# Three PSUM banks for the scores and two for the row maxima, in place of two and three

## The chip, the core and the metric

The kernel runs on one NeuronCore of a Trainium2 chip. The metric is the device time of one execution in microseconds (us). TensorE multiplies matrices and writes its results into PSUM, which has eight banks of 128 partitions by 512 fp32 values. VectorE (DVE in the profile) and ScalarE (ACT) read the results from there; GpSimd (POOL) works on SBUF alone, and SyncE (SP) issues nearly all DMAs. Each engine takes its instructions in one fixed order, and waits on semaphores for the others.

## What is computed

One step of a small hybrid decoder: one recurrent layer, then one attention layer ("FoX", attention with a forget term) on 2048 new prompt tokens, and the same for 8 sequences of 8 sampled tokens with 4096 cached positions each. The attention has 16 heads of 64 dimensions. All values are fp32. Cut to the attention:

```python
def fox_block(q, k, v, cq, ck, q_pos, k_pos):
    s = jnp.einsum('bqhd,bkhd->bhqk', q, k).astype(jnp.float32) * (HEAD_DIM ** -0.5)
    s = s + jnp.swapaxes(cq, 1, 2)[:, :, :, None] - jnp.swapaxes(ck, 1, 2)[:, :, None, :]
    mask = k_pos[None, :] <= q_pos[:, None]
    s = jnp.where(mask[None, None], s, -jnp.inf)
    p = jax.nn.softmax(s, axis=-1)
    return jnp.einsum('bhqk,bkhd->bqhd', p.astype(v.dtype), v)
```

`c` is the running sum of the log-forget values. The result is gated with `silu(g)`, multiplied with the output weights, normalized and added to the residual.

## The kernel before

**Stages.** Up to about 1240 us of the span the recurrent layer and the first half of the projections to queries, keys, values and gates run; up to about 1705 us come the other projections, beside the decode attention over the cached pages. From about 1705 us to 2842 us the prompt's attention runs (`attention`), and until about 2725 us the rest of the decode attention runs beside it, its pages streaming in from the cache. Then the last rows of the output projection end the program.

**The prompt's attention.** The work is cut into 64 units: one head `h` and one block `qc` of 512 queries, with qc running 0, 1, 2, 3 in even heads and 3, 2, 1, 0 in odd ones. A unit has 4(qc+1) tiles of 128 keys by 512 queries. For each unit:

- Row maxima first (`top`, L1405 to L1422). For each 128 queries and each block of 512 keys TensorE writes approximate scores, queries on the partitions, into a PSUM tile `sx` (L1415, one fp32r matmul of up to 512 columns). DVE reduces it to one maximum for each query: L1417 for whole blocks, L1419 with a mask on the diagonal. When a unit's last `sx` is reduced, DVE takes the maximum over the blocks (L1428), TensorE transposes the four columns into a PSUM tile `mps` (L1432), and ACT writes them, negated, in four steps as rows 96 to 99 of the query operand `qbt` (L1434).
- Scores (L1552 to L1555). For each tile of 128 keys TensorE adds up in a PSUM tile `st`: L1552 with `qa`, `ka`, which needs no maxima; L1553 with `qbt`, `kbt`, which brings in the forget term and subtracts the row maxima, so that it needs the unit's L1434; and L1555, the causal mask, on the diagonal. ACT takes the exponential (L1561) into `p`, or into `acc` for the first tile.
- Products with the values (L1572, `ops`), for four tiles together; POOL adds the `p` tiles into `acc` (L106) for the sums of the softmax.
- `total` (L1465, PSUM tile `tot`) sums `acc` over the partitions, and `norm` and `gate` (L1489, PSUM tile `rp`) scale and gate the result and send it to DRAM (`ogd`).

**The decode beside it.** For a page of keys, SP's queue brings `raw` (L1083), DVE transposes it (L1168, `ktr`), TensorE forms scores (L1136, `dS`) and DVE subtracts and reduces; for a page of values TensorE multiplies (L1246, `dO`). It has two PSUM banks of its own, tags `d` and `o`.

**PSUM.** The attention's pool has six banks: one for `ops`, two under the tag `st`, three under the tag `sx`. The tag `sx` serves `sx`, `mps`, `tot` and `rp` in turn. A tile that takes a bank waits until its last owner has been read. Once the decode is done (`dec_done`), `scores_bank` (L1536) takes every other score tile from the decode's two banks, so that there are four in turn.

**The order.** The program is written as generators that call each other. `advance` (L1507) writes the maxima tiles some 18 ticks, of one score tile each, ahead of the scores that need them, and `Side` deals out the decode's steps along the attention's. That is not the order of the engines, though: the framework's scheduler plays the program through on a clock of its own, and puts an instruction into its engine's order when its inputs and its buffer are free there. The number of banks thus sets the order. `behind` (L110) keeps the transposes of L1168 behind the last row maximum on DVE, and the products `dS` and `dO` behind the last score matmul on TensorE.

**The last rows.** `project` (L1617) multiplies 17 blocks of rows with the output weights. Even blocks take their two PSUM tiles `y` from the decode's banks, odd ones from the tag `st` (L1661).

Of the kernel before, what the change touches and what calls it, by code (L numbers as in the profile page):

```python
# [11 lines left out]
F32 = mybir.dt.float32  # L12
# [73 lines left out]
def tile_hawk_fox(  # L86
# [1231 lines left out]
    def attention(es):  # L1318
# [1 line left out]
        ps3 = psum["att"]  # L1320

        ops2 = ps3.tile([P, 512], F32, name="ops", tag="ops", bufs=1)
        ps3.tile([P, 512], F32, name="st", tag="st", bufs=2)
        pool.tile([P, 512], F32, name="acc", tag="acc", bufs=NACC)
        pool.tile([P, 512], F32, name="p", tag="p", bufs=NP)
        pool.tile([P, 512], F32, name="oT", tag="oT", bufs=5)
# [78 lines left out]
        def top(u, j, ck):  # L1405

            h, qc = units[u]
            assert h in loaded and u < done[1]
            kb, qb = kbs[h % 2], qbs[u % NQ]
            if (j, ck) == (0, 0):  # L1410
                mxs[u] = small.tile([P, 4, 4], F32, name="mxs", tag="mxs")
            mx = mxs[u]
            w = 512 if ck < qc else (j + 1) * P
            ps = ps3.tile([P, 512], F32, name="sx", tag="sx", bufs=3)
            T.matmul(ps[:, :w], qb[0:96, j * P:(j + 1) * P], kb[0:96, ck * 512:ck * 512 + w], start=True, stop=True)  # L1415
            if ck < qc:
                place["V"] = V.reduce_max(mx[:, j, ck:ck + 1], ps[:, :w], axis=AX.X).ins  # L1417
            else:
                V.tensor_tensor_reduce(ps[:, :w], ps[:, :w], maskb[:, 512 - w:], scale=1.0, scalar=NEG,  # L1419
                                       op0=ALU.add, op1=ALU.max, accum_out=mx[:, j, ck:ck + 1])  # L1420
            if j == 3 and ck == qc:
                later.after(1, lambda: tops(u))  # L1422

        def tops(u):

            h, qc = units[u]
            m = mrows[u % 2]
            V.tensor_reduce(m[:, :4], mxs.pop(u)[:, :, :qc + 1], axis=AX.X, op=ALU.max)  # L1428

            def row():  # L1430
                ps = ps3.tile([P, 512], F32, name="mps", tag="sx", bufs=3)
                T.transpose(ps[:, :P], m[:, :], ident[:, :])  # L1432
                for j in range(4):
                    A.mul(qbs[u % NQ][96:100, j * P:(j + 1) * P], ps[:4, :P], less[:, j:j + 1])  # L1434

            later.after(1, row)
# [23 lines left out]
        def total(h2, sums, todo, single):  # L1460


            ps = ps3.tile([P, 512], F32, name="tot", tag="sx", bufs=3)
            for qc, acc in todo:
                T.matmul(ps[qc * 32:(qc + 1) * 32, :], ones[:, :32], acc[:, :], start=True, stop=True)  # L1465
            cs = pool.tile([P, 512], F32, name="cs", tag="cs")
            rows = slice(0, P) if len(todo) == 4 else slice(qc * 32, (qc + 1) * 32)
            A.copy(cs[rows, :], ps[rows, :])
            if single:
                for qc, acc in todo:  # L1470
                    j = qc * 2 + h2
                    S.dma_start(sums[j * 16:(j + 1) * 16, :], cs[qc * 32:qc * 32 + 1, :].rearrange("o (r c) -> o r c", r=16))
            else:
                S.dma_start(sums[h2 * HD:(h2 + 1) * HD, :], cs[:, :].rearrange("(q z) (r c) -> z q r c", z=32, r=16)[0])

        def norm(pr, sums, q0, n, oT):

            ps_ = slice(q0 * 32, (q0 + n) * 32)
            V.reciprocal(sums[ps_, :], sums[ps_, :])
            rs = [pool.tile([P, 32], F32R, name=f"rs{x}", tag=f"rs{x}") for x in range(2)]  # L1480
            V.tensor_copy(rs[0][ps_, :], sums[ps_, :])
            tt(V, rs[1][ps_, :], sums[ps_, :], f(rs[0][ps_, :]), ALU.subtract)
            for x in range(2):
                to = rr[x * 8:(x + 1) * 8, :] if n == 4 else rr[x * 8 + q0:x * 8 + q0 + 5:4, :]
                S.dma_start(f(to).rearrange("j (r c) -> j r c", r=16), f(rs[x][ps_, :]))

            def gate(qc, sg):
                ps = ps3.tile([P, 512], F32, name="rp", tag="sx", bufs=3)
                T.matmul(ps[:, :], sel[:, qc, :], rr[:, :], start=True, stop=True)  # L1489
                tt(G, sg[:, :], sg[:, :], oT[qc - q0][:, :], ALU.mult)  # L1490
                tt(V, sg[:, :], sg[:, :], ps[:, :], ALU.mult)
                S.dma_start(og_d[qc][pr * P:(pr + 1) * P, :], sg[:, :])

            def fetch(qc):
                sg = pool.tile([P, 512], F32, name="sgt", tag="sgt", bufs=2)
                S.dma_start(sg[:, :], sg_d[pr * P:(pr + 1) * P, qc * 512:(qc + 1) * 512])
                later.after(3, lambda: gate(qc, sg))

            for qc in range(q0, q0 + n):
                later.after((3 if n == 4 else 0) + 2 * (qc - q0), lambda qc=qc: fetch(qc))  # L1500
# [35 lines left out]
        def scores_bank():  # L1536

            if dec_done:
                wide[0] += 1
                if wide[0] % 2:  # L1540
                    return psum["dec"].tile([P, 512], F32, name="st", tag="do"[wide[0] // 2 % 2], bufs=1)
            return ps3.tile([P, 512], F32, name="st", tag="st", bufs=2)

        for u, (h, qc) in enumerate(units):
            load_low(u + 2)
# [71 lines left out]
    def project(es):  # L1617

        bpostB, out = proj["g"], proj["out"]

        def tiled(t):
            return t.rearrange("p (k t) -> p k t", k=KB)

        def gated_rows(i, og):
            m, t, res, _ = rows[i]
            if t is None:
                tt(V, og[:, :, :m], oTs[:, :, :], sgs[:, :, :], ALU.mult)
            else:
                S.dma_start(og[:, :, :], og_d[t // 512][:, t % 512:t % 512 + P].rearrange("(k p) t -> p k t", p=P))

        def residual(i, x1):
            m, t, res, _ = rows[i]
            S.dma_start(x1[:m, :], res)

        def split(i, og, oh, ol):
            m = rows[i][0]
            cp(A, oh[:, :, :m], og[:, :, :m])
            tt(V, ol[:, :, :m], og[:, :, :m], f(oh[:, :, :m]), ALU.subtract)

        def post(i, pool, yps, x1, y):  # L1640
            m, t, res, dst = rows[i]
            ss = sumsq(pool, yps, m)
            r = rsqrt(ss[:m], m, 0.25 / D, post=0.5)
            for j in range(2):
                sl = slice(j * 512, (j + 1) * 512)
                V.scalar_tensor_tensor(y[:m, sl], yps[j][:m, :], r[:m, 0:1], bpostB[:m, sl], op0=ALU.mult, op1=ALU.mult)
                tt(V if i == len(rows) - 1 and j == 1 else G, y[:m, sl], y[:m, sl], x1[:m, sl], ALU.add)
                if i == len(rows) - 1:
                    S.dma_start(dst[:, sl], y[:m, sl])
            if i < len(rows) - 1:  # L1650
                S.dma_start(dst, y[:m, :])

        pool = sbuf(es, "proje", "right")
        hs = lent["halves"]()
        sets = [dict(og=pool.tile([P, KB, P], F32, name="ogT"), x1=pool.tile([P, D], F32, name="x1"),
                     oh=pool.tile([P, KB, P], F32R, name="ohT"), ol=pool.tile([P, KB, P], F32R, name="olT"),
                     y=pool.tile([P, D], F32, name="yo"),
                     ps=lambda j: psum["dec"].tile([P, 512], F32, name="y", tag="do"[j], bufs=1)),
                dict(og=tiled(lent["res"][:, :D]), x1=lent["res"][:, D:], oh=tiled(hs[:, :D]), ol=tiled(hs[:, D:]),
                     y=lent["out"][:, :, :].rearrange("p k d -> p (k d)"),  # L1660
                     ps=lambda j: lent["psum"].tile([P, 512], F32, name="y", tag="st", bufs=2))]  # L1661

        def part(i, fn, *names):
            if i < len(rows):
                fn(i, *(sets[i % 2][n] for n in names))

        for i in range(2):
            part(i, gated_rows, "og")
            part(i, residual, "x1")
        part(0, split, "og", "oh", "ol")  # L1670
        for i in range(len(rows)):
            b = sets[i % 2]
            yps = []
            for j in range(2):
                ps = b["ps"](j)
                out.product(ps, rows[i][0], j, b["oh"], b["ol"])
                yps.append(ps)
                if j == 0:
                    part(i + 2, gated_rows, "og")
                    part(i + 1, split, "og", "oh", "ol")  # L1680
            post(i, pool, yps, b["x1"], b["y"])
            part(i + 2, residual, "x1")
            if i == 3:
                later.flush()
# [175 lines left out]
```

## Time and profile before

| | us |
|---|---|
| median of 3 runs (3048.39 to 3065.48) | 3050.73 |
| the profiled execution | 3044.43 |
| its span, first to last instruction | 3042.6 |
| TensorE busy in the span | 2818.0 (93%) |
| DVE busy | 1801.1 (59%) |
| ACT busy | 1271.1 (42%) |
| POOL busy | 1080.0 (35%) |
| attention beside the decode, 1705 to 2725 us: span / TensorE busy | 1020.0 / 939.6 |
| attention alone, 2725 to 2842 us | 117.0 / 110.4 |
| last rows, from 2842 us | 200.6 / 190.9 |

The profile is one execution. A matmul's time in a row is its way through the array, and matmuls follow each other faster than that; the distance of two starts says how long one holds TensorE. "PEld" is the load of a matmul's stationary operand, which overlaps the matmuls before it. "PEclk" is the TensorE clock that was granted, as a share of full speed. "idle before <- X" is the time that an engine stood idle before a group, and what ended it. Some fp32 matmuls are shown as two.

### The profile page before, as it was taken

To read this page: it belongs to the slowest core of one execution; us is meant where nothing else is said; L and a number is where in the kernel's file an instruction comes from. 1 tells how busy PE (TensorE), PEld (TensorE's weight loads), DVE (VectorE), ACT (ScalarE), POOL (GpSimd) and SP (SyncE) were. 2 spreads that over 40 slices of the span, in tenths; PEclk is the share of its full clock that TensorE was granted. 3 is DMA by queue.
4 is the path that set the end of the run, shared out by engine and by line. 5 is a ranking of instruction groups with operands and counts; after the bars stand their busy time and mean duration, and the time that the engine had idled before them with its cause. 6 is when DMAs were issued, how large, how long until landed. Compare 5 with 4: busy or idle time off the path is not lost.

```text
span 3042.6 us, 60436 instructions
## 1 busy us (share of the span) xinstructions
PE 2818.0 (93%) x21614; PEld 2260.3 (74%) x21614; DVE 1801.1 (59%) x4012; ACT 1271.1 (42%) x2874; POOL 1080.0 (35%) x1199
## 2 busy tenths in 40 slices
PE   5998999999999989998999799899999999999998
PEld 5997789989899978896788455556655656556687
DVE  7876455425357765766555566666666766555344
ACT  4665442222236654433244144344434444355321
POOL 1653201000015532000000265556665666558422
PEclk9999999999999999999999799999999999999999
DMA  4224546788622265999999978898889898974343
GB/s 122 84 83 133 176 123 197 241 263 265 223 91 79 84 195 176 302 327 323 327 311 325 276 229 258 259 273 260 267 270 282 253 278 258 276 232 117 96 146 109
DMA packets 492862, 653.39 MB, mean 215 GB/s; under 512 B 91099, under 2 KB 292828, under 8 KB 485285
## 3 DMA queue, kind: packets, MB, share of 16 engines
q1 hardware_dynamic: 488934, 643.87, 67.8%
q10 hardware_dynamic: 3340, 3.56, 0.5%
q8 instruction: 171, 2.80, 0.4%
q0 software_dynamic: 288, 2.10, 0.2%
q14 instruction: 129, 1.06, 0.1%
HBM read 513.82 MB, written 135.16 MB: 213 GB/s over the span
## 4 chain that ended last, share of the span: by engine, by line
PE 51%; DMA 15%; DVE 6%; ACT 4%; SPq 4%; issue 3%; POOL 1%; ACTq 0%; DVEq 0%; POOLq 0%
PE ops L1572 7%; PE st L1552 4%; PE sx L1415 4%; DMA raw<-in_cache_k_dram 3%; PE dO L1246 3%; PE y L379 3%; PE y L378 3%; PE y L377 3%; PE kv L378 3%; PE kv L377 3%; PE st L1553 3%; PE kv L379 3%; PE dS L1136 3%; DMA raw<-in_cache_v_dram 3%; SPq L1083 2%
## 5 line engine op out<-in xcount | busy, mean ns | idle before, releaser
L106 POOL TENSOR_TENSOR acc<-acc,p 128x512 f32<-128x512 f32 (+3 forms) x576 | 639.7, 1112 | 408.2 <-PE ops L1572 220.6
L1561 ACT ACTIVATE p<-st 128x512 f32<-128x512 f32 (+3 forms) x576 | 291.5, 525 | 398.0 <-PE st L1553 183.9
L1168 DVE STREAM_TRANSPOSE ktr<-raw 128x1024 f32<-128x1024 f32 x256 | 308.0, 1226 | 107.2 <-DMA raw<-in_cache_k_dram 94.4
L1417 DVE TENSOR_REDUCE mxs<-sx 128x1 f32<-128x512 f32 x384 | 254.1, 681 | 183.2 <-PE sx L1415 182.0
L378 PE MATMUL kv<-wl,xh 128*128 128x256 f32 (+3 forms) x1088 | 310.0, 288 | 9.4 <-DVE wl L422 9.3
L377 PE MATMUL kv<-wh,xh 128*128 128x256 f32 (+3 forms) x1088 | 310.5, 290 | 6.9 <-ACT wh L421 6.6
L379 PE MATMUL kv<-wh,xl 128*128 128x256 f32 (+3 forms) x1088 | 309.8, 287 | 0.0
L1552 PE MATMUL st<-qa,ka 128*128 128x512 f32 (+3 forms) x640 | 273.1, 427 | 12.6 <-ACT p L1561 10.9
L1572 PE MATMUL ops<-p,vvt 128*64 128x256 f32 (+1 forms) x2176 | 269.1, 374 | 3.8 <-ACT p L1561 3.6
L1415 PE MATMUL sx<-kbt,qbt 96*128 96x512 f32 (+3 forms) x640 | 233.9, 421 | 34.8 <-DVE mxs L1419 12.7
L421 ACT ACTIVATE wh<-wst,gv 128x256 fp32r<-128x256 f32 (+1 forms) x384 | 164.3, 499 | 184.4 <-DMA wst<-in_b_w_in_dram 69.9
L1553 PE MATMUL st<-qbt,kbt 128*128 128x512 f32 (+3 forms) x640 | 238.1, 373 | 0.0
L422 DVE SCALAR_TENSOR_TENSOR wl<-wst,gv,wh 128x256 fp32r<-128x256 f32 (+1 forms) x384 | 170.2, 493 | 113.5 <-ACT wh L421 110.3
L1572 PEld LDWEIGHTS ops<-p,vvt 128*64 128x64 f32 x2176 | 165.0, 143 | 91.7 <-issue 22.2
L377 PE MATMUL qg<-xh,wh 128*128 128x384 f32 (+2 forms) x640 | 228.3, 358 | 0.0
L379 PE MATMUL qg<-xh,wl 128*128 128x384 f32 (+2 forms) x640 | 226.7, 355 | 1.1 <-DVE wl L422 1.1
L378 PE MATMUL qg<-xl,wh 128*128 128x512 f32 (+2 forms) x640 | 226.6, 356 | 0.0
L378 PEld LDWEIGHTS kv<-wl,xh 128*128 128x128 f32 (+1 forms) x1088 | 204.0, 189 | 13.9 <-DVE wl L422 10.9
L1101 POOL TENSOR_TENSOR qw<-qb,amask 128x128 f32<-128x128 f32 x64 | 29.4, 463 | 518.1 <-PE dS L1136 276.6
L377 PEld LDWEIGHTS kv<-wh,xh 128*128 128x128 f32 (+1 forms) x1088 | 203.8, 189 | 11.9 <-ACT wh L421 7.5
L379 PEld LDWEIGHTS kv<-wh,xl 128*128 128x128 f32 (+1 forms) x1088 | 205.7, 190 | 4.1 <-issue 3.9
L1552 PEld LDWEIGHTS st<-qa,ka 128*128 128x128 f32 x640 | 125.1, 196 | 107.4 <-issue 54.6
(297 smaller groups left out, 6346.4 us busy)
## 6 DMA issues: line engine op xcount, KB each, us to landing
raw<-in_cache_k_dram SPq DMA_DIRECT2D x512, 256.0 KB
raw<-in_cache_v_dram SPq DMA_DIRECT2D x512, 256.0 KB
wst<-in_w_kv_dram SPq DMA_DIRECT2D x48, 512.0 KB
wst<-in_b_w_in_dram SPq DMA_DIRECT2D x48, 512.0 KB
xt<-in_x_prompt_dram SPq DMA_DIRECT2D x32, 512.0 KB
wst<-in_a_w_in_dram SPq DMA_DIRECT2D x64, 256.0 KB
out_dram<-kf SPq DMA_DIRECT2D x128, 128.0 KB
sc<-cd SPq DMA_DIRECT2D x16, 1024.0 KB
```

What stands on the lines that cost most here:

```text
L106: eng.tensor_tensor(out, a, b, op=op)
L377: T.matmul(ps, lh(k), rh(k), start=(k == 0), stop=False)
L378: T.matmul(ps, lh(k), rl(k), start=False, stop=False)
L379: T.matmul(ps, ll(k), rh(k), start=False, stop=(k == nk - 1))
L422: V.scalar_tensor_tensor(wl[:, k, :], st[:, k, :], gk, f(wh[:, k, :]), op0=ALU.mult, op1=ALU.subtract)
L1168: behind("V", V.transpose(t.kts[pp][:, n], raw[:, :, pp * 256:(pp + 1) * 256]).ins)
L1415: T.matmul(ps[:, :w], qb[0:96, j * P:(j + 1) * P], kb[0:96, ck * 512:ck * 512 + w], start=True, stop=True)
L1417: place["V"] = V.reduce_max(mx[:, j, ck:ck + 1], ps[:, :w], axis=AX.X).ins
L1552: place["T"] = T.matmul(ps[:, lo:], ka[:, ks], qa[:, lo:], start=True, stop=False).ins
L1553: T.matmul(ps[:, lo:], kb[:, ks], qb[:, lo:], start=False, stop=(k < qc * 4))
L1561: pair.append((k, lo, p, A.activation(p[:, lo:], ps[:, lo:], AF.Exp)))
L1572: return T.matmul(ops[r * HD:(r + 1) * HD, a0 * P:], vvs[h % 2][:, k, :], p[:, :].rearrange("p (a r c) -> p a r c", a=2, r=2)[:, a0:, r, : ...
```

## The change

The attention's six banks are dealt out anew: three under the tag `st`, two under the tag `sx`. So that the number of score banks after the decode stays four, `scores_bank` then takes every fourth tile from the decode's bank `d`, and no more from `o`. The odd blocks of the last rows turn through three banks and no longer two.

```diff
@@ attention
-        ps3.tile([P, 512], F32, name="st", tag="st", bufs=2)
+        ps3.tile([P, 512], F32, name="st", tag="st", bufs=3)
@@ top
-            ps = ps3.tile([P, 512], F32, name="sx", tag="sx", bufs=3)
+            ps = ps3.tile([P, 512], F32, name="sx", tag="sx", bufs=2)
@@ tops, row; total and gate have the same for "tot" and "rp"
-                ps = ps3.tile([P, 512], F32, name="mps", tag="sx", bufs=3)
+                ps = ps3.tile([P, 512], F32, name="mps", tag="sx", bufs=2)
@@ scores_bank
                 wide[0] += 1
-                if wide[0] % 2:
-                    return psum["dec"].tile([P, 512], F32, name="st", tag="do"[wide[0] // 2 % 2], bufs=1)
-            return ps3.tile([P, 512], F32, name="st", tag="st", bufs=2)
+                if wide[0] % 4 == 0:
+                    return psum["dec"].tile([P, 512], F32, name="st", tag="d", bufs=1)
+            return ps3.tile([P, 512], F32, name="st", tag="st", bufs=3)
@@ project
-                     ps=lambda j: lent["psum"].tile([P, 512], F32, name="y", tag="st", bufs=2))]
+                     ps=lambda j: lent["psum"].tile([P, 512], F32, name="y", tag="st", bufs=3))]
```

No instruction is added or removed. The orders of the engines in the attention are others, since the scheduler made them anew with the new banks. The rows below are TensorE's order. `qbt_19530` to `qbt_19535` are the six query operands that the units take in turn, so that a name's number tells the unit; two score rows (L1552, L1553) with one `qbt` are one tile of that unit's scores.

The first place is the beginning of the unit of head 12 with qc = 2, whose operand is `qbt_19532`. Before:

```order
L1415 MATMUL sx<-kbt_19529,qbt_19533 128x512 x2
L1415 MATMUL sx<-kbt_19529,qbt_19533 128x384
L1552 MATMUL st<-qa,ka 128x128
L1553 MATMUL st<-qbt_19531,kbt_19529 128x128
L1555 LDWEIGHTS identB
L1555 MATMUL st<-causal,identB 128x128
L1552 MATMUL st<-qa,ka 128x512
L1553 MATMUL st<-qbt_19532,kbt_19529 128x512
L1415 MATMUL sx<-kbt_19529,qbt_19533 128x512
```

After:

```order
L1553 MATMUL st<-qbt_19531,kbt_19529 128x128
L1555 LDWEIGHTS identB
L1555 MATMUL st<-causal,identB 128x128
L1552 MATMUL st<-qa,ka 128x512
L1415 MATMUL sx<-kbt_19529,qbt_19532 128x512 x3
L1432 MATMUL mps<-ident,mrow_19567 128x128
L1415 MATMUL sx<-kbt_19529,qbt_19533 128x512 x2
L1553 MATMUL st<-qbt_19532,kbt_19529 128x512
L1415 MATMUL sx<-kbt_19529,qbt_19533 128x512
```

Before, the unit's first L1553 follows its L1552 at once, and the maxima tiles around it belong to the next unit, 19533. Now the unit's own last three maxima tiles and the transpose of its maxima stand between its L1552 and its L1553.

The second place is the beginning of the unit of head 11 with qc = 3, operand `qbt_19532` with the keys `kbt_19537`, beside which the decode's `dS` and `dO` run. Before:

```order
L1552 MATMUL st<-qa,ka 128x128
L1553 MATMUL st<-qbt_19531,kbt_19529 128x128
L1555 LDWEIGHTS identB
L1555 MATMUL st<-causal,identB 128x128
L1246 MATMUL dO<-raw,sx 32x256 x8
L1415 MATMUL sx<-kbt_19537,qbt_19533 128x512
L1552 MATMUL st<-qa,ka 128x512
L1553 MATMUL st<-qbt_19532,kbt_19537 128x512
L1136 MATMUL dS<-ktr,qw 32x128 x32
```

After:

```order
L1552 MATMUL st<-qa,ka 128x512
L1415 MATMUL sx<-kbt_19537,qbt_19532 128x512 x2
L1415 MATMUL sx<-kbt_19537,qbt_19532 128x384
L1415 MATMUL sx<-kbt_19537,qbt_19532 128x512 x4
L1136 MATMUL dS<-ktr,qw 32x128 x32
L1432 MATMUL mps<-ident,mrow_19567 128x128
L1415 MATMUL sx<-kbt_19537,qbt_19533 128x512
L1246 MATMUL dO<-raw,sx 32x256 x8
L1151 MATMUL dS<-sy,qw 32x8 x16
L1415 MATMUL sx<-kbt_19537,qbt_19533 128x512
L1415 MATMUL sx<-kbt_19537,qbt_19533 128x128
L1553 MATMUL st<-qbt_19532,kbt_19537 128x512 x3
```

The seven last maxima tiles of the unit, which stood more than thirty rows ahead of its scores, have moved down to just before them, seven in a row on two banks. The first halves of three score tiles stand above them (the third is the first row shown), and their three second halves together below.

More of the change, by code (lines that the diff above doesn't have):

```diff
@@ L1460, in total @@
         def total(h2, sums, todo, single):
-            ps = ps3.tile([P, 512], F32, name="tot", tag="sx", bufs=3)
+            ps = ps3.tile([P, 512], F32, name="tot", tag="sx", bufs=2)
             for qc, acc in todo:
@@ L1487, in gate @@
             def gate(qc, sg):
-                ps = ps3.tile([P, 512], F32, name="rp", tag="sx", bufs=3)
+                ps = ps3.tile([P, 512], F32, name="rp", tag="sx", bufs=2)
                 T.matmul(ps[:, :], sel[:, qc, :], rr[:, :], start=True, stop=True)
```

## The prediction

> **What bounds the kernel now.** I read the head of the page first, then the busy time by stage, and then, in the stage of the change, the waits of TensorE, because an engine that is busy for 93% of the span can only be slowed or sped by what it waits for.
>
> ```profile
> span 3042.6 us, 60436 instructions
> PE 2818.0 (93%) x21614; PEld 2260.3 (74%) x21614; DVE 1801.1 (59%) x4012; ACT 1271.1 (42%) x2874; POOL 1080.0 (35%) x1199
> ```
>
> The execution took 3044.43 us around this span. The median of the three runs is 6.3 us more.
>
> ```profile
> core 0: us, PE busy (x) PEld busy (x) DVE busy (x) ACT busy (x) POOL busy (x), PEclk, DMA share, GB/s
> 1705.00:1724.00 19.00, 11.05 (x23) 6.01 (x24) 11.40 (x32) 2.11 (x8) 2.23 (x5) 0.50 1.08 293
> 1724.00:2725.00 1001.00, 928.54 (x8457) 593.08 (x8457) 636.41 (x1341) 437.33 (x1086) 585.50 (x563) 0.95 0.86 263
> 2725.00:2842.00 117.00, 110.38 (x653) 69.02 (x652) 58.34 (x117) 68.99 (x146) 101.79 (x85) 0.97 0.39 107
> 2842.00:3042.60 200.60, 190.87 (x829) 151.14 (x827) 83.00 (x266) 39.47 (x87) 47.07 (x39) 0.99 0.38 122
> ```
>
> The attention beside the decode (1724 to 2725 us) is the stage that counts. TensorE stands idle there for 1001 - 928.5 = 72.5 us. The granted clock is 0.95 on average; as it reads 0.50 in the first row and near 1 in the last, I take it that half speed held for about a tenth of the stage, some 100 us, which cost 50 us of work. DVE is at 64%, ACT at 44%, the DMA at 0.86. What TensorE waited for in this stage:
>
> ```profile
> PE dO L1246 <- DMA raw<-in_cache_v_dram: 19.9, 10, 5.2
> PE sx L1415 <- DVE mxs L1419: 12.4, 11, 5.1
> PE st L1552 <- ACT p L1561: 10.9, 24, 2.3
> PE rp L1489 <- DMA r<-rs: 4.7, 3, 2.7
> PE mps L1432 <- DVE mrow L1428: 4.3, 4, 2.7
> PE sx L1415 <- DVE mxs L1417: 4.2, 8, 1.0
> ```
>
> The banks of the scores cost 10.9 us (L1552 waits until an exponential has freed one), and the banks of the maxima 12.4 + 4.2 = 16.6 us. A wait on a `qbt` before L1553, the point at which the maxima reach the scores, is not among the rows: with three banks the maxima are ready in time. So the first prize is small, and the question is what the third bank of the maxima was worth.
>
> **The price of a maxima tile.** This is one round trip, from the order of time:
>
> ```profile
> 2029.78 0.50 PE L1415 MATMUL sx<-kbt,qbt 96*128 96x512 f32 x1
> 2030.12 0.40 PE L1552 MATMUL st<-qa,ka 128*128 128x512 f32 x1
> 2030.35 1.95 DVE L1417 TENSOR_REDUCE mxs<-sx 128x1 f32<-128x512 f32 x3
> 2030.36 0.39 PE L1553 MATMUL st<-qbt,kbt 128*128 128x512 f32 x1
> 2030.59 0.63 PE L1415 MATMUL sx<-kbt,qbt 96*128 96x512 f32 x2
> 2030.85 0.60 ACT L1561 ACTIVATE p<-st 128x512 f32<-128x512 f32 x1 [0.21 <-PE st L1553]
> ```
>
> ```profile
> L1417 DVE TENSOR_REDUCE mxs<-sx 128x1 f32<-128x512 f32 x384 | 254.1, 681 | 183.2 <-PE sx L1415 182.0
> L1168 DVE STREAM_TRANSPOSE ktr<-raw 128x1024 f32<-128x1024 f32 x256 | 308.0, 1226 | 107.2 <-DMA raw<-in_cache_k_dram 94.4 <-DMA qa<-qd 4.4 <-issue 3.8
> ```
>
> A 512-wide matmul holds TensorE for 0.23 us (from 2030.36 to 2030.59). The reduction starts 0.57 us after its matmul and takes 0.68, so a bank comes back 1.25 us after the matmul's start at the earliest, and later by 1.23 us for every transpose of L1168 that stands ahead on DVE. Of three maxima tiles in a row on two banks the third is due at 0.46 us and waits 0.79; each further one waits for DVE's pace, 0.68 - 0.23 = 0.45.
>
> **Part 1: maxima tiles close behind the last owner of their bank.** I went through TensorE's order before and after, bank by bank, and summed the work between the last write of a bank's owner and the first of the next (0.23 us for 512 columns, 0.24 for a product's pair of rows). Before, 20 maxima tiles have less than 0.3 us between, and 50 have 0.3 to 0.9; after, 101 and 80, and ten more `tot` and `rp` tiles stand right behind maxima. So 81 + 10 new waits of between 0.45 and 0.79 us: 41 to 72 us. I take 0.6, since most are in runs of three or four: 55 us. For the 30 of the middle class the same arithmetic gives 0 to 0.7 us each, 0 to 20; I take 0.27, as much of this distance was already covered before (the 16.6 us were all that 70 close tiles cost): 8 us. Queued behind such a tile is all of TensorE: the scores for which ACT waits, and `dS` and `dO`, which free the page buffers that SP's loads wait for.
>
> **Part 2: the maxima come just in time.** This is what the third score bank does to the order. A score tile's first half (L1552) needs no maxima, so with a free bank it goes ahead, and the maxima tiles, short of banks, fall back. Between a unit's last `sx` and its first L1553 stood a median of 16.7 us of TensorE work, 3.3 at the least. Now it is 5.3, and under 2.9 in 16 of 64 units; in 29 units (3 before) less than 1.4 us stand between `mps` and L1553, and in 10 (4 before) less than 1.4 between the last `sx` and `mps`. What this distance must hold:
>
> ```profile
> 2018.35 0.68 DVE L1419 CUSTOM_DVE_ANT_0 sx<-sx,maskb 128x512 f32<-128x512 f32 x1
> 2018.95 0.13 DVE L1419 DVE_READ_ACCUMULATOR2_ANT mxs<- 128x1 f32 x1
> 2019.12 0.17 DVE L1428 TENSOR_REDUCE mrow<-mxs 128x4 f32<-128x12 f32 x1
> ```
>
> ```profile
> 2024.54 0.33 PE L1432 MATMUL mps<-ident,mrow 128*128 128x128 f32 x1
> 2024.90 1.11 ACT L1434 ACTIVATE qbt<-mps,less 4x128 fp32r<-4x128 f32 x4 [1.80 <-PE mps L1432]
> ```
>
> From a tile's start to its maximum in `mrow` it is 0.57 + 0.94 = 1.5 us (1.3 after TensorE is done with it), and from `mps` to the last write of `qbt` 2026.01 - 2024.54 = 1.47. What is missing to 1.4 us, summed over the units, is 1.2 us before and 21.2 after at `mps` to L1553, and 2.9 and 12.9 at `sx` to `mps`: 30 us more. The bounds are 0, if TensorE is late there anyway, and about 50, if the four writes of L1434 stand behind an exponential of 0.60 us each time (29 x 0.6 = 17). I take 30.
>
> **Part 3: the scores' banks.** Score tiles with less than 0.5 us of work since their bank's last owner fall from 34 to 15. All that can be gained is the 10.9 us; I take 7.
>
> **Part 4: what the DMA waits give back.** A later TensorE finds its pages there: of the 19.9 + 4.7 us of DMA waits I take half, 12; bounds 0 and 24.6.
>
> **Part 5: the clock.** A wait costs more than its length here:
>
> ```profile
> 2012.08 1.94 PE L1415 MATMUL sx<-kbt,qbt 96*128 96x384 f32 x3 [1.87 <-DVE mxs L1419]
> ```
>
> ```profile
> 2012.60:2022.80 10.20, 10.17 (x69) 7.23 (x73) 6.87 (x15) 2.18 (x6) 2.79 (x3) 0.50 0.91 258
> ```
>
> After this wait of 1.87 us for a maxima bank the clock stood at 0.50 for 10.2 us, with TensorE busy all along: 5 us more. Over the stage it is 50 us lost for 72.5 us idle, 0.7 for each; the new waits are shorter than that one, so I take 0.3 of the 55 + 8 + 30 - 7 - 12 = 74 us: 22. The bounds are 0 and 0.7 x 74 = 52.
>
> The Trainium skill, page "TensorE: Matmul & The Clock Gate", section "Loop structure matters more than you think", has reading a result out of PSUM as something that doesn't make TensorE go cold; by that the term would be 0 and the sum 22 us smaller. The row at 2012.08 disagrees, as the wait was for just such a read.
>
> **Edits at nothing.** After the decode, four score banks turn before and after; TensorE is busy for 110.4 of 117 us there, and this rotation hides the exponential equally. The unused bank `o` is missed by nobody until `project` takes it. In the last rows the third bank could only touch the idle 200.6 - 190.9 = 9.7 us, and the next tile's 24 matmuls (5.5 us) cover the reads.
>
> **Sum.** 55 + 8 + 30 - 7 - 12 + 22 = 96 us. Against the profiled execution that is 3044 + 96 = 3140 us, against the median 3147; I name 3140.
>
> **Rivals.**
>
> *The scores' bank decides.* Faster: ACT's waits on scores are the longest of its own, so a third bank might let TensorE run ahead. For it speaks that ACT and DVE both idle longest for TensorE:
>
> ```profile
> ACT p L1561 <- PE st L1553: 179.9, 130, 7.0
> DVE mxs L1417 <- PE sx L1415: 158.2, 95, 7.2
> ```
>
> Against it: both rows say that they wait for TensorE, not it for them. Its price is the 10.9 us at L1552 and, at 0.7, 8 of clock: 3044 - 19 = 3025 us. It decides if the maxima tiles' banks come back in time all the same, that is if parts 1 and 2 realise less than 19 us.
>
> *Hidden behind the page stream.* If the pages at a DMA share of 0.86 set the pace, TensorE's new waits fall into those for pages. Parts 1 and 2 then shrink by the whole 24.6 us, and cost their lower ends, 41 + 0 + 0, with no clock term: 3044 + 41 - 7 - 25 = 3053 us, up to 3065. Against it: pages account for only about 20 of the 72.5 us idle.
>
> *The clock falls.* If every wait counts as the one at 2012.08, with lost work 2.7 times the wait (5 / 1.87), on half of the 93 us of parts 1 and 2: 0.5 x 93 x 2.7 = 126 us in place of 22, and 3244 us. For it speaks that row; against it that the stage's mean is 0.7.
>
> The Trainium skill's same page describes this in the section "A second HAM failure mode: psum-queue depth-cycling": turning through PSUM banks leaves small idle gaps, and the clock swings between half and full. The 3244 us is this rule at work.
>
> **Chances.** The forecast 0.62; hidden 0.17; the clock falls 0.13; the scores' bank decides 0.08. My forecast's own terms reach from 3044 + 41 - 11 - 25 = 3049 to 3044 + 72 + 20 + 50 + 52 = 3238. The range leaves out the faster rival, the lower half of the hidden one and the clock's far end: 3060 to 3215. A measurement of this kernel can tell about 0.5% (15 us) from no change. Faster than 3035 is the first rival alone, 0.08; within 3035 to 3066 lies a little over half of the hidden one, 0.09; the rest, 0.83, is slower.
>
> **What the profile of the changed kernel would show.** Part 1: `sx` waiting on `mxs` goes from 16.6 us to over 50. Part 2: a row of L1553 waiting on `qbt` of L1434 appears, with 15 us or more, and `mps` waiting on `mrow` grows past 10. Part 3: L1552 waiting on `p` falls below 8 us. Part 4: `dO` waiting on `raw` falls. Part 5: PEclk in the stage falls below 0.94. The last rows keep their 200 us. I would be wrong if the waits at L1415 stayed near 17 us, or if they came and the page waits went by the same amount.

## The result, and the profile after

The changed kernel takes 3186.68 us (median of 4 runs, 3171.68 to 3191.84) against 3049.56 us of the kernel before on the same chip. The ratio is 1.0441, with a 95% interval of 1.0412 to 1.0469: it is 137 us slower. The profiled executions differ by 3169.8 - 3042.6 = 127 us of span, and the readings below account for those.

The head of the page after, and the busy time by stage. The decode now ends at about 2837 us and the attention at about 2970 us; these stages answer to 1724 to 2725, 2725 to 2842 and 2842 to 3042.6 us before.

```profile
span 3169.8 us, 60453 instructions
PE 2857.9 (90%) x21614; PEld 2269.9 (72%) x21614; DVE 1810.9 (57%) x4012; ACT 1260.2 (40%) x2874; POOL 1076.6 (34%) x1199
```

```profile
core 0: us, PE busy (x) PEld busy (x) DVE busy (x) ACT busy (x) POOL busy (x), PEclk, DMA share, GB/s
1724.00:2837.00 1113.00, 966.10 (x8444) 605.57 (x8437) 637.58 (x1324) 424.69 (x1080) 586.91 (x564) 0.91 0.78 236
2837.00:2970.00 133.00, 118.13 (x656) 72.76 (x657) 68.97 (x137) 66.75 (x145) 91.29 (x81) 0.92 0.28 78
2970.00:3169.80 199.80, 189.86 (x829) 150.25 (x829) 85.32 (x268) 42.17 (x93) 50.78 (x42) 0.99 0.41 133
```

The attention beside the decode is 112 us longer, the attention alone 16 us, the last rows are as before. In the first of these stages TensorE's idle time went from 72.5 to 1113 - 966.1 = 146.9 us. The granted clock fell from 0.95 to 0.91; read as a share of time at half speed, this is 1001 x 0.05 = 50 us of work lost before and 1113 x 0.09 = 100 us after. With the 74 us of new idle time this adds up to 124 us, for 112, so the clock's part is too large as read: half-speed time in which TensorE was idle anyway counts in it. The busy time measures it better: with the same matmuls it grew by 966.1 - 928.5 = 37.6 us, and 74.4 + 37.6 is 112.

TensorE's waits after the change, from 1724 to 2837 us (total us, times, longest):

```profile
PE dO L1246 <- DMA raw<-in_cache_v_dram: 51.1, 26, 7.7
PE sx L1415 <- DVE mxs L1417: 23.8, 44, 1.2
PE dS L1136 <- DVE ktr L1168: 13.5, 7, 3.6
PE mps L1432 <- DVE mrow L1428: 11.6, 11, 2.2
PE sx L1415 <- DVE mxs L1419: 8.8, 15, 1.2
PE sx L1415 <- DVE sgt L106: 6.6, 3, 3.0
PE dO L1246 <- DMA sx<-pd: 4.9, 2, 4.3
PE sx L1415 <- ACT qbt L1434: 4.7, 7, 1.0
PE tot L1465 <- DVE mxs L1417: 3.4, 5, 1.2
...
PE st L1552 <- ACT p L1561: 2.2, 4, 1.3
```

Of the same list before, three rows that the prediction did not show:

```profile
PE dS L1136 <- DVE ktr L1168: 2.6, 4, 1.2
...
PE sx L1415 <- DVE sgt L106: 1.4, 2, 0.9
...
PE sx L1415 <- ACT qbt L1434: 0.8, 2, 0.6
```

The waits for a maxima bank (the `sx` and `tot` rows shown here and in the prediction) went from 4.2 + 12.4 + 1.4 + 0.8 = 18.8 us to 23.8 + 8.8 + 6.6 + 4.7 + 3.4 = 47.3. No single wait of `sx` or `tot` on `mxs` is longer than 1.2 us; there are many, 74 in the five rows where 23 were. `mps` rose by 7.3, value pages by 31.2, transposed keys by 10.9; L1552 gained 8.7. So less than half of the new idle time stands at the maxima's banks, and more at the page stream, though the DMA share fell from 0.86 to 0.78: the pages are late without the transfers being busier. What SP's queue waited for before it could issue page loads (L1083) shows where they start late; before and then after, in the same stage:

```profile
SPq L1083 <- PE dO L1246: 27.9, 11, 4.7
```

```profile
SPq L1083 <- PE dO L1246: 46.3, 24, 4.0
```

A load waits until a product has freed its page buffer, and TensorE's product is late. On ACT, L1434 waits longer for `mps`, and the exponentials wait less for their scores; in the same stage before:

```profile
ACT p L1561 <- PE st L1555: 160.9, 101, 6.6
...
ACT qbt L1434 <- PE mps L1432: 44.0, 23, 7.2
```

and after:

```profile
ACT qbt L1434 <- PE mps L1432: 146.8, 31, 18.2
ACT p L1561 <- PE st L1553: 138.0, 88, 4.5
...
ACT p L1561 <- PE st L1555: 96.7, 63, 6.8
```

L1434 waits 103 us more, and the two rows of the exponentials (L1553 was 179.9 us before) 106 us less. ACT's idle time has changed its place; that the late maxima hold up exponentials which are ready is not shown by it.

### The profile page after: what moved, and what is told of

Its sections match the earlier page's. It is cut to its first block, busy times and chain, and to the rows that moved or that the text cites. A ratio compares the mean times of both kernels' runs of the same rounds, so it can differ in the third digit from the quotient of the medians.

```text
span 3169.8 us, 60453 instructions
## 1 busy us (share of the span) xinstructions
PE 2857.9 (90%) x21614; PEld 2269.9 (72%) x21614; DVE 1810.9 (57%) x4012; ACT 1260.2 (40%) x2874; POOL 1076.6 (34%) x1199
## 4 chain that ended last, share of the span: by engine, by line
PE 49%; DMA 18%; DVE 8%; SPq 3%; ACT 3%; issue 3%; POOL 1%; ACTq 0%; DVEq 0%; POOLq 0%
PE ops L1572 6%; DMA raw<-in_cache_v_dram 5%; PE st L1552 4%; PE sx L1415 3%; PE dO L1246 3%; PE st L1553 3%; PE y L377 3%; PE dS L1136 3%; PE y L379 3%; PE y L378 3%; DMA raw<-in_cache_k_dram 3%; PE kv L377 3%; PE kv L378 3%; PE kv L379 3%; SPq L1083 2%
## 5 line engine op out<-in xcount | busy, mean ns | idle before, releaser
L1561 ACT ACTIVATE p<-st 128x512 f32<-128x512 f32 (+3 forms) x576 | 283.2, 526 | 344.1 <-PE st L1553 146.7
L1417 DVE TENSOR_REDUCE mxs<-sx 128x1 f32<-128x512 f32 x384 | 258.9, 684 | 222.5 <-PE sx L1415 220.3
L1415 PE MATMUL sx<-kbt,qbt 96*128 96x512 f32 (+3 forms) x640 | 268.8, 452 | 68.5 <-DVE mxs L1417 30.8
L1572 PE MATMUL ops<-p,vvt 128*64 128x256 f32 (+1 forms) x2176 | 264.2, 370 | 2.5 <-ACT p L1561 2.4
L1552 PE MATMUL st<-qa,ka 128*128 128x512 f32 (+3 forms) x640 | 260.9, 416 | 5.0 <-ACT p L1561 2.7
L1415 PEld LDWEIGHTS sx<-kbt,qbt 96*128 96x128 f32 x640 | 128.5, 209 | 164.4 <-DVE mxs L1417 66.6
L1553 PE MATMUL st<-qbt,kbt 128*128 128x512 f32 (+3 forms) x640 | 228.1, 379 | 0.0
L1572 PEld LDWEIGHTS ops<-p,vvt 128*64 128x64 f32 x2176 | 162.4, 141 | 90.2 <-issue 20.6
L1246 PE MATMUL dO<-raw,sx 128*32 128x256 f32 x2048 | 151.6, 420 | 74.3 <-DMA raw<-in_cache_v_dram 53.6
```

Of the source, the lines that this page charges most:

```text
L1246: return T.matmul(op[c:c + 32, :256], sx[:, d, i // 4, a * 4:(a + 1) * 4, :].rearrange("p h q -> p (h q)"), raw[:, d, a * 256:(a + 1) * 25 ...
L1552: place["T"] = T.matmul(ps[:, lo:], ka[:, ks], qa[:, lo:], start=True, stop=False).ins
L1553: T.matmul(ps[:, lo:], kb[:, ks], qb[:, lo:], start=False, stop=(k < qc * 4))
L1561: pair.append((k, lo, p, A.activation(p[:, lo:], ps[:, lo:], AF.Exp)))
L1572: return T.matmul(ops[r * HD:(r + 1) * HD, a0 * P:], vvs[h % 2][:, k, :], p[:, :].rearrange("p (a r c) -> p a r c", a=2, r=2)[:, a0:, r, : ...
```

## The experiments

Theory A says that the order does it: the third score bank lets the scores' first halves go ahead, and the maxima fall behind. Theory B says that the round trip of a maxima bank does it: two banks are too few whatever the order. The medians of the timed runs, and the loss of each changed kernel against its own base, are:

| kernel | us | ratio to the kernel before (95%) | loss against its base |
|---|---|---|---|
| changed | 3186.7 | 1.0441 (1.0412 to 1.0469) | 137 |
| two score banks, two maxima banks | 3197.0 | 1.0484 (1.0441 to 1.0527) | 144 |
| before, order held | 3097.4 | 1.0157 (1.0109 to 1.0206) | |
| changed, order held | 3183.2 | 1.0424 (1.0377 to 1.0471) | 86 |
| before, half reduction | 3028.3 | 0.9927 (0.9898 to 0.9956) | |
| changed, half reduction | 3142.8 | 1.0305 (1.0263 to 1.0348) | 115 |
| before, no decode beside | 2750.7 | 0.9016 (0.8981 to 0.9052) | |
| changed, no decode beside | 2805.7 | 0.9200 (0.9171 to 0.9229) | 55 |
| changed, bank `o` to the maxima after the decode | 3186.8 | 1.0438 (1.0405 to 1.0472) | 135 |
| before, transposes cut | 3064.4 | 1.0053 (1.0028 to 1.0079) | |
| changed, transposes cut | 3172.3 | 1.0421 (1.0378 to 1.0465) | 108 |
| before, half of the value pages | 3033.0 | 0.9949 (0.9930 to 0.9969) | |
| changed, half of the value pages | 3176.0 | 1.0421 (1.0372 to 1.0470) | 143 |

**The maxima bank taken away, nothing given.** On the kernel before:

```diff
-tag="sx", bufs=3
+tag="sx", bufs=2        (sx, mps, tot and rp)
```

> The kernel before with the third maxima bank taken away and nothing given to the scores (two and two, the sixth bank of the pool idle). Theory A, the order: the loss comes from maxima that fall behind because the scores' first halves go ahead into a third bank. Without that bank the first halves stand apart from their second halves in 26 of 64 units (6 before the change, 53 after it), so the loss should be about half: 3100 to 3140 us. Theory B, the round trip: two maxima banks are too few in any order, and the third score bank gained 8 us; the time should be that of the changed kernel and those 8 us: 3185 to 3205 us.

It took 3197.0 us. The whole loss comes from the maxima's bank, as B said, and the third score bank is worth about 10 us, which is within the intervals; the expected 8 us fit. A's figure of 3100 to 3140 us falls, and with it A's mechanism as the main one: first halves stand ahead far less often here (in 26 of 64 units against 53, as the expectation counts them), and the loss was no smaller.

**The order held.** On the changed kernel, and as a control on the kernel before:

```diff
-T.matmul(ps[:, :w], qb[0:96, j * P:(j + 1) * P], ...)
+place["X"] = T.matmul(ps[:, :w], qb[0:96, j * P:(j + 1) * P], ...).ins
...
 place["T"] = T.matmul(ps[:, lo:], ka[:, ks], qa[:, lo:], start=True, stop=False).ins
+behind("X", place["T"])
```

> The changed kernel (three score banks, two maxima banks) with TensorE's order held: a score tile's first half may not stand ahead of the maxima tiles that the program wrote before it. The median distance from a unit's last maxima tile to its first second half is then 25 us of TensorE's work (16 before the change, 5 after it); maxima tiles within 0.3 us of their bank's last owner are 64 (21 before, 103 after), within 0.3 to 0.9 us 250 (57 and 88). Theory A, the order: most of the loss is back, 3050 to 3090 us, and the waits for pages are near those of before (20 us). Theory B, the round trip: the close tiles still wait, and 250 middling ones with them: 3150 us or more.

> The kernel before (two score banks, three maxima banks) with the same hold on TensorE's order; the median distance is 27 us in place of 16. The control for the held order alone. Theory A: the distance was enough already, so no change or a little less: 3030 to 3060 us. Theory B: the maxima tiles' own waits do not change (13 close tiles in place of 21): 3040 to 3060 us. Over 3070 us would say that the hold costs something by itself, and the other held run is then to be read against this one.

The changed kernel with the order held, 3183.2 us, lies where B expected it and far above A's 3050 to 3090. But the hold costs 44 us by itself (3097.4 us, outside what both theories expected), so the two runs are read against each other: 86 us are lost with the order held, 137 without. The changed kernel with the order held waited on TensorE, from 1724 to 2845 us, for:

```profile
PE sx L1415 <- DVE mxs L1417: 46.6, 69, 8.2
PE sx L1415 <- DVE mxs L1419: 25.0, 29, 3.0
PE sx L1415 <- DVE sgt L106: 23.0, 11, 13.6
PE dS L1136 <- DVE ktr L1168: 6.7, 4, 5.3
```

```profile
1724.00:2845.00 1121.00, 984.80 (x8430) 608.69 (x8431) 640.85 (x1344) 434.25 (x1087) 585.43 (x563) 0.91 0.76 234
```

The kernel before with the order held, from 1724 to 2770 us:

```profile
PE sx L1415 <- DVE sgt L106: 9.1, 5, 3.4
PE sx L1415 <- DVE mxs L1417: 8.6, 17, 1.2
...
PE sx L1415 <- DVE mxs L1419: 6.2, 7, 2.9
```

```profile
1724.00:2770.00 1046.00, 943.00 (x8428) 591.95 (x8428) 639.08 (x1343) 437.24 (x1083) 586.11 (x563) 0.94 0.82 251
```

With the order held, taking the bank away raises these three rows from 23.9 to 94.6 us, and the idle time from 103 to 136. Against the changed kernel in its own order, the 51 us of waits for value pages are gone (3.3 us are left), the waits at the maxima's banks have doubled, and the idle time and the clock (0.91) are nearly the same. So the page waits there do not look like a cost of their own: where the maxima come in time, TensorE waits at their banks in their place. By this pair 51 of the 137 us go with the free order, and since the hold is no free edit, this is not a clean measure of the maxima that fell behind.

**DVE's part of the round trip halved.** On both kernels:

```diff
-V.reduce_max(mx[:, j, ck:ck + 1], ps[:, :w], axis=AX.X)
+V.reduce_max(mx[:, j, ck:ck + 1], ps[:, :w // 2], axis=AX.X)
```

> The changed kernel with DVE's reduction of a whole block of maxima (L1417) over the first 256 of its 512 columns; what is left out is the other half of the maxima, so that a row's maximum may be too small by what stands there. A reduction should take about 0.36 us in place of 0.68. Theory B, the round trip: a bank comes back 0.3 us sooner, the waits of maxima tiles for DVE halve (33 to 16 us), and with the clock the time falls to 3130 to 3160 us. Theory A, the order: the distance stays (5.4 us against 5.0), so the pages stay late: 3165 to 3190 us.

> The kernel before with the halved reduction of L1417 (the second half of each whole block's maxima is left out): the control of the same edit on the changed kernel, which gained 44 us there. Theory B: with three banks the maxima tiles wait 21 us in all, half of that and its clock can go: 3030 to 3045 us. If it gains 40 us here too, to 3010 us, that gain was DVE's load and not the banks.

The halved reduction took 0.417 us in place of 0.684, not the 0.36 I had expected:

```profile
L1417 DVE TENSOR_REDUCE mxs<-sx 128x1 f32<-128x256 f32 x384 | 157.4, 417 | 212.9 <-PE sx L1415 211.4
```

The changed kernel gained 44 us, as B expected. The kernel before gained 23.6, which is 2 us past B's range: over half of the 44 us come with three banks too, and are DVE's lighter load and not the missing bank. The loss between the two fell from 137 to 115 us. That fits a shorter round trip that gives back a part of what a bank was worth, but the difference of 22 us stands against intervals of about 9 us on the 137, and 13 and 9 on the two runs. The kernel before with this edit, at 3028.3 us, is the fastest here of those that leave nothing of the decode out, and ahead of both kernels by more than the interval. A softmax does not depend on the value that is subtracted, as long as the exponentials stay in range; a kernel that used this would have to know that of its scores.

**Without the decode beside.** On both kernels:

```diff
+G.memset(oTs[:, :, :], 0.0)
...
-yield from decode(dec, turns[FIRST:], 4, 2, True)
+yield from decode(dec, turns[FIRST:FIRST + 3], 4, 2, True)
 dec.close()
-dec_done.append(True)
```

> The kernel before without the decode beside the attention: of 14 decode turns only the first three run, before the attention begins; eleven turns' pages, transposes and products, and their part of the sampled rows' result, are left out, and the scores stay on their own two banks to the end. It is the base for the next run, and says nothing alone; about 2750 to 2850 us.

> The changed kernel with the same eleven turns left out, three score banks and two maxima banks to the end. Theory B, the round trip of a maxima bank: it needs no pages; with less other work of TensorE between them the maxima tiles stand even closer (94 within 0.3 us of their bank's last owner and 146 within 0.9, against 7 and 88 in the run before it), so it is 40 us or more slower than that run. Theory C, the pages: the loss comes from the page stream, which a late TensorE starves; without pages it is within 15 us of that run.

Without pages or transposes the change still costs 55 us, as B said; C, that the page stream makes the loss, falls as the whole cause. The waits of TensorE in the attention, before (1724 to 2563 us; the attention's lines have numbers that are one higher in these runs):

```profile
PE st L1553 <- ACT p L1562: 9.7, 23, 1.6
...
PE sx L1416 <- DVE mxs L1418: 0.5, 3, 0.2
```

and with the change (1724 to 2606 us):

```profile
PE sx L1416 <- DVE mxs L1418: 25.6, 43, 0.8
PE mps L1433 <- DVE mrow L1429: 8.4, 8, 1.1
PE sx L1416 <- ACT qbt L1435: 8.1, 21, 0.5
PE st L1553 <- ACT p L1562: 4.5, 8, 1.3
```

Here no page and no transpose is in the way: with three banks L1416 waits 0.5 us for maxima of whole blocks in all, with two 25.6, and 8.4 more in the chain behind a unit's last tile. The stage's busy rows, before and after:

```profile
1724.00:2563.00 839.00, 807.66 (x4703) 504.42 (x4698) 394.94 (x963) 444.06 (x1008) 656.76 (x594) 0.99 0.33 85
```

```profile
1724.00:2606.00 882.00, 820.66 (x4698) 514.69 (x4697) 414.86 (x971) 439.39 (x1006) 651.75 (x592) 0.95 0.31 80
```

Of 43 us, 30 are idle time (31.3 to 61.3); the clock fell from 0.99 to 0.95, which is 36 us of work by the same reading as above, in large part inside the idle time: TensorE's busy time grew by 13.0 us.

**The tail.** On the changed kernel, once the decode is done:

```diff
+def maxima_bank(name):
+    if dec_done:
+        turn_o[0] += 1
+        if turn_o[0] % 3 == 0:
+            return psum["dec"].tile([P, 512], F32, name=name, tag="o", bufs=1)
+    return ps3.tile([P, 512], F32, name=name, tag="sx", bufs=2)
```

> The changed kernel with the decode's idle bank o given to every third tile of the maxima (and the transposes and sums that share their banks) once the decode is done: three maxima banks in the last 135 us of the attention, where the change lost 18 us. Theory B: most of the 18 us come back, 3168 to 3178 us. If the tail is longer because it began late, by work moved into it, nothing changes: 3182 to 3190 us.

3186.8 us: nothing changed in the total. The tail of its profile is 130 us, against 133 after and 117 before, so the missing bank by itself is not what makes the tail 16 us longer, or no more than a few us of it. By the rows of the stage, 8 of the 16 us are idle time (6.6 to 14.9) and the clock there fell from 0.97 to 0.92. In the changed kernel the new idle time does stand at the maxima: L1415 on L1417 went from 0.3 to 5.5 us there. With the third bank that row fell to 1.9, but L1572 and the scores then waited for exponentials (7.1 us in place of 1.7), and the idle time stayed at 13.3. What set this off stays open.

**Transposes cut in two.** On both kernels:

```diff
-behind("V", V.transpose(t.kts[pp][:, n], raw[:, :, pp * 256:(pp + 1) * 256]).ins)
+for i in range(0, 4, 2):
+    behind("V", V.transpose(t.kts[pp][:, n, i:i + 2], raw[:, i:i + 2, pp * 256:(pp + 1) * 256]).ins)
```

> The changed kernel with DVE's page transposes (L1168, 1.23 us each) cut into two of 512 columns each, about 0.63 us, so that a reduction of maxima can come between the halves. Without the decode the change cost 55 us, with it 137; this asks whether the other 82 us come from transposes that stand ahead of reductions and hold a maxima bank longer. Theory D, DVE's queue: then a bank comes back up to 0.6 us sooner beside each transpose, and the time falls by 15 us or more, to 3150 to 3172 us. If the 82 us have other causes (less work of TensorE free to stand between, late pages, the clock): 3178 to 3200 us.

> The kernel before with the same cut transposes, as a control: three maxima banks wait 21 us in all, so the cut is worth little there: 3035 to 3055 us under each theory. If it gains as much as the changed kernel does, the cut helps the decode and not the banks.

The changed kernel took 3172.3 us, at the edge of theory D's range, and its interval reaches over the uncut kernel's; the control lost 13 us, and so came out above its range. The loss between them is 108 us for 137, a difference of 29 us with intervals of about 13 us on the one and 8 on the other, and 13 of the 29 us are the control's loss. A half took 0.67 us (median), so DVE has more work in both. Transposes ahead of reductions may be a part of the loss; this does not show it.

**Half of the value pages.** On both kernels two of four pages are loaded, and each is used twice:

```diff
-for i in range(4):
+for i in range(4 if cache is cache_k else 2):
...
-raw[:, d, a * 256:(a + 1) * 256]
+raw[:, d % 2, a * 256:(a + 1) * 256]
```

> The kernel before with only two of each four value pages loaded, and used twice; half of the value pages is left out (a quarter of the cached bytes), and the sampled rows' result with it. All instructions of the engines stay. It is the base for the next run; the 20 us of waits for value pages should mostly go: 3010 to 3045 us.

> The changed kernel with the same half of the value pages left out. Theory C, in part: the change adds 31 us of waits for value pages and 11 for transposed keys by itself, on top of the waits of the maxima's banks; with the pages early they go and are not replaced, and the loss against the run before it falls from 137 to 100 us or less. Theory B alone: the waits for pages only stand where others would (holding the order moved them from pages to the maxima's banks with the same sum), so the loss stays at 120 us or more, with more waits at the maxima's banks.

The loss stayed, at 143 us, with a quarter of the cached bytes gone. The kernel before came out in its range, but its waits for value pages, which I had thought would mostly go, hardly fell from 19.9 us (1724 to 2700 us):

```profile
PE dO L1246 <- DMA raw<-in_cache_v_dram: 17.2, 8, 6.9
```

The first rows of the changed one's waits:

```profile
PE dO L1246 <- DMA raw<-in_cache_v_dram: 33.9, 13, 6.5
PE sx L1415 <- DVE mxs L1417: 22.5, 40, 1.2
PE dS L1136 <- DVE ktr L1168: 14.1, 7, 3.6
PE mps L1432 <- DVE mrow L1428: 13.1, 10, 2.5
```

The waits for pages fell from 51 to 34 us, what the change adds to them from 31 to 17, and the loss did not fall, so the volume of the value pages is not its cause. With the held order, where they all but vanished and the idle time stayed, this speaks for their following from TensorE being late. More page buffers, which would test it from the other side, were not tried.

## Why the prediction was right, and where it was not

The direction and the mechanism held: a maxima bank is worth more than a score bank, because its round trip over DVE is what TensorE then waits for. That the bank itself is worth it is shown by the run that takes it away and gives nothing (144 us), and the waits at it by the pair without the decode. The time lies in the range, and the sum was 96 us where the profiles show 127 and the medians 137. Its terms:

- **Part 1, close maxima tiles: 63 us forecast, 28.5 measured** at the banks in the stage. The sign that I gave, `sx` on `mxs` past 50 us, did not come: it is 23.8 + 8.8 = 32.6. The size of a wait was right, 23.8 us over 44 waits or 0.54 each for L1417; their number was not. The rows have 74 waits for 23 before, 51 more, where I counted 91 + 30 tiles. A tile that stands close in the order need not wait if TensorE was held up anywhere in between. That this is the reason is not shown.
- **Part 2, the maxima just in time: 30 us forecast, 7.3 measured,** all of it at `mps`. The wait of L1553 on `qbt`, of which I had said 15 us or more, does not appear among the rows. A likely reason is that maxima tiles stand between `mps` and L1553 and wait for their own banks, and that those waits cover ACT's four writes; no run isolates it. The fallen maxima show on ACT instead, where L1434 waited 103 us longer and the exponentials less.
- **Part 3, the scores' bank: -7 forecast, -8.7 measured.** The two-and-two run gives about 10 us from the other side, which is within the intervals.
- **Part 4, the DMA waits: -12 forecast; value pages +31.2, probability rows (`sx` of `pd`) +4.9, transposed keys +10.9, and -4.7 at `rp`.** This is the step that failed, with its sign: "A later TensorE finds its pages there." The pages are not on a clock of their own. Their loads wait for a buffer that a product frees, and SP's wait for that rose from 27.9 to 46.3 us; a late TensorE makes late pages. The two runs that bear on it (order held, half of the value pages) fit this reading, and neither proves it.
- **Part 5, the clock: 22 us forecast, 38 measured** as the growth of TensorE's busy time; read off the granted clock, the way the prediction did it, it is 50. The factor of 0.3 was too small: 38 us for 74 us of new idle time is 0.5, and 50 us is 0.7, which I had as the upper bound. I had discounted it because the new waits are short. They are, and the clock fell all the same, from 0.95 to 0.91.
- **The tail, at nothing: 16 us.** I had named the rotation of four score banks as the cover, and not asked about the maxima's banks, of which the tail too has one less. The rows of the changed kernel show TensorE waiting there, but the run that gives the third bank back shows no shorter time.

So what was too large (parts 1 and 2, by 57 us) offset the larger part of what was too small or of the wrong sign (part 4 by 54, part 5 by 16, the tail by 16). That the sum came within 31 us of the profiles is in good part luck.

On the two rules that the prediction weighed: the Trainium skill, page "TensorE: Matmul & The Clock Gate", section "Loop structure matters more than you think", has a copy out of PSUM leave TensorE's clock alone where the next matmuls follow immediately. Here they did not, as TensorE waited for the read with two banks, and the granted clock was 0.95 against 0.99 in the pair without the decode. The rival that drew on the section "A second HAM failure mode: psum-queue depth-cycling" had the right cause, short idle gaps from turning through PSUM banks, at too high a price: 126 us forecast, 38 to 50 measured.

Of the other rivals, the scores' bank did not decide (10 us), and the page stream hid nothing. What stays open is why the loss is 137 us with the decode and 55 without it. The volume of the value pages is out; the transposes on DVE are a candidate for 29 us at most, and no run leaves the decode's work on DVE out alone; the rows show where the rest stands (pages, transposed keys and the clock) but not what it would be without the maxima's waits.

## What to carry to other kernels

When PSUM banks are dealt out between two streams, compare the round trips: how long after a matmul's start its reader gives the bank back, and what else that reader's queue holds; the longest waits of the readers for TensorE said nothing on it here. An engine that is late at one place can be late wherever its own progress frees buffers, so that a wait may turn up at a transfer which is not slow, as with the pages here at a falling DMA share. And where the clock falls after idle time, a wait costs more than its length. For each us of new idle time TensorE's busy time over the same matmuls grew by 0.5 us with the change (37.6 for 74.4), by 0.4 without the decode (13.0 for 30.0) and by 1.3 with the order held (41.8 for 33.2).

## What the runs showed of the hardware

Short waits are enough to lower the clock. The changed kernel without the decode dropped to half speed for 10.2 us at a turn between two heads, and did so seven times from 1827 to 2506 us, about every 113 us, at every second turn. One such place, in order of time; the longest idle gap is 1.05 us:

```profile
2048.42 1.03 PE L1416 MATMUL sx<-kbt,qbt 96*128 96x512 f32 x2
2049.71 0.50 PE L1416 MATMUL sx<-kbt,qbt 96*128 96x512 f32 x1 [0.26 <-DVE mxs L1418]
2051.26 0.33 PE L1433 MATMUL mps<-ident,mrow 128*128 128x128 f32 x1 [1.05 <-DVE mrow L1429]
2051.34 0.48 PE L1416 MATMUL sx<-kbt,qbt 96*128 96x512 f32 x1
2052.61 0.80 PE L1416 MATMUL sx<-kbt,qbt 96*128 96x512 f32 x1 [0.78 <-DVE mxs L1418]
```

```profile
2042.00:2052.00 10.00, 7.70 (x31) 4.48 (x31) 7.54 (x18) 4.50 (x12) 1.09 (x2) 1.00 0.65 135
2052.00:2062.20 10.20, 8.62 (x25) 3.79 (x27) 5.24 (x11) 2.29 (x6) 0.30 (x1) 0.50 0.01 2
2062.20:2072.00 9.80, 9.80 (x62) 6.45 (x58) 4.64 (x10) 4.79 (x10) 9.41 (x9) 1.00 0.03 4
```

TensorE was busy for 77% of the 10 us ahead of the drop, for 84% of the 10.2 us at half speed, and the clock came back. How much clock an idle us costs was not the same everywhere: read off the granted clock it was 50 us for 72.5 idle in the kernel before, but only 8 for 31.3 without the decode. The other surprise is DVE's reduction: half the columns took 0.417 us of 0.684, so that, if its time grows evenly with the columns, the part which does not depend on them is about 0.417 - (0.684 - 0.417) = 0.15 us (an estimate from these two sizes).
